# Moving three sums of raw weight blocks per set from VectorE to GpSimd in a seven-product matmul

## The chip, the cores and the metric

The kernel runs on one core of a Trainium2 chip. The metric is the device time in microseconds (us) of one execution. Three timed runs of the kernel before gave 2255.5, 2255.51 and 2257.45 us; the median is 2255.51 us. One more execution was taken by the hardware profiler.

## The reference, cut to what matters

One layer of a hybrid decoder on 256 rows of width 2048: a SwiGLU feed-forward block (FFN), a token mixer, a second FFN, each between RMS norms. The change touches only the two FFNs:

```
def swiglu(x, w_gate, w_up, w_down):
    return (jax.nn.silu(x @ w_gate) * (x @ w_up)) @ w_down      # D_FF = 5504 = 43 tiles of 128

h = swiglu(rms_norm(x, ffn1_pre[l]), ffn1_wg[l], ffn1_wu[l], ffn1_wd[l])
x = x + 0.5 * rms_norm(h, ffn1_post[l])
```

All is float32. The weights come from HBM once each.

## The kernel before, in words

Every product of float32 matrices is made of three TensorE products of rounded halves: the weight block is split into `hi` (ScalarE, line 170, a rounding copy) and `lo` (VectorE, line 171, raw minus `hi`), and the matmul adds x_hi·hi, x_hi·lo and x_lo·hi. So each raw tile of 128x1024 that a DMA brings costs one ScalarE instruction, one VectorE instruction and 6 or 12 matmuls. The raw tiles rotate through 12 buffers (`N_RAW`), `hi` and `lo` through 5 buffers each (`N_SPLIT`): ScalarE and VectorE can run ahead of TensorE by no more than 5 tiles.

Most of each FFN is a main stream (`main`, `linear_steps`, lines 315 to 318) of ordinary products. Into it `weave` threads a side stream (`sevens`) at `RATIO` 0.5: after each batch of main matmuls come 6 side matmuls. The side stream computes four blocks of gate columns and one block of up columns of each FFN, ten groups in the kernel, by Strassen's scheme: x and W are cut in 2x2 blocks, and seven block products replace eight. Sums of blocks of x are made once (`new_forms`). Sums of blocks of W must be made as the weights arrive.

A group has two phases, each over four sets s = 0..3 (a set is two rows of 128 of the contraction). Phase one takes products 1 and 2, on plain blocks. Phase two loads three raw tiles per set, r[0], r[1], r[2] (blocks 11, 12 and 22 of W), on SP's queue (`loads`, line 412) and takes five products. Each product is written s-wise, and a sort key `5*s + d` sets the order: 3(s), 5(s), 4(s-1), 6(s), 7(s). Their operands:

- 3(s): r[2] as loaded
- 5(s): r[0] + r[1], summed into r[0]
- 6(s): that plus r[2], summed into r[0] once 5(s) has been split
- 7(s): r[2] + r[1], summed into r[2]
- 4(s): r[0] of 6(s) plus block 21, added by a DMA with accumulation that GpSimd's queue issues (`t4`, line 454), once 6(s) has been split

The three sums are the function `add`, line 398, on VectorE: 3 per set, 12 per group, 120 in the kernel. The set after the current one is always being loaded (`while len(got) < ...`).

Within the program order the tile framework fixes each engine's queue before the run: it lists instructions by priority (program order) and by when it estimates that their operands are ready. So a sum whose tiles are estimated to have landed can stand in its engine's queue ahead of work of an earlier phase. The queue is then taken strictly in order on the chip. GpSimd's queue holds, in this stretch, the DMAs of `t4` and the DMAs that write partial sums of the down product (lines 648 and 650).

Of the kernel before, what the change touches and what calls it, by code (L numbers as in the profile page):

```python
# [14 lines left out]
ALU = mybir.AluOpType  # L15
# [41 lines left out]
def layer(ctx: ExitStack, tc: tile.TileContext, a, out: bass.AP):  # L57
    nc = tc.nc
    V, S, G, PE = nc.vector, nc.scalar, nc.gpsimd, nc.tensor
# [12 lines left out]
    def slot(shape, dt=F32, s="s"):  # L72
        return pool.tile(shape, dt, tag="slot", bufs=N_SLOT, name=nm(s))
# [10 lines left out]
    def acc(w):  # L84
        return psp.tile([P, 512], F32, tag="bank", bufs=N_BANK, name=nm("acc"))[:, :w]
# [82 lines left out]
    def split(hi, lo, src):  # L168

        S.activation(hi, src, AF.Copy)  # L170
        V.tensor_tensor(lo, src, f32(hi), ALU.subtract)  # L171
# [19 lines left out]
    def raw_tile():  # L191
        return pool.tile([P, 1024], F32, tag="raw", bufs=N_RAW, name=nm("raw"))

    def split_tiles():
        return (pool.tile([P, 1024], F32R, tag="whi", bufs=N_SPLIT, name=nm("whi")),
                pool.tile([P, 1024], F32R, tag="wlo", bufs=N_SPLIT, name=nm("wlo")))
# [193 lines left out]
    def sevens(forms, groups, done):  # L390

        a, b = slice(0, 512), slice(512, 1024)
        fetch, got = [], []

        def add(x, y):
            V.tensor_tensor(x, x, y, ALU.add)  # L398
            return x

        def source(W, col):
            def src(i, j, s):
                k = 8 * i + 2 * s
                return W[k * P:(k + 2) * P, col + 512 * j:col + 512 * j + 512].rearrange("(k p) c -> p k c", p=P)

            return src

        def loads(src, blocks, s):
            tiles = []
            for i, j in blocks:  # L410
                x = raw_tile()
                nc.sync.dma_start(out=x.rearrange("p (k c) -> p k c", c=512), in_=src(i, j, s))
                tiles.append(x)
            return tiles

        for _, W, col, _ in groups:
            for blocks in (((0, 0), (1, 0)), ((0, 0), (0, 1), (1, 1))):
                for s in range(4):
                    fetch.append((source(W, col), blocks, s))

        def phase(first, plan):

            bank = {}
            seen = {p: 0 for p, _, _ in plan}
            for _, p, s, operand in sorted((len(plan) * s + d, p, s, o) for s in range(4) for p, d, o in plan):
                while len(got) < min(first + s + 2, len(fetch)):
                    got.append(loads(*fetch[len(got)]))
                x = operand(s, got[first + s])
                hi, lo = split_tiles()
                split(hi, lo, x)  # L430
                if p not in bank:
                    bank[p] = acc(512)
                ah, al = forms[p]
                for i in range(2):
                    k, ws = 2 * s + i, slice(512 * i, 512 * i + 512)
                    PE.matmul(bank[p], ah[:, k, :], hi[:, ws], start=(seen[p] == 0), stop=False)  # L436
                    PE.matmul(bank[p], ah[:, k, :], lo[:, ws], start=False, stop=False)  # L437
                    PE.matmul(bank[p], al[:, k, :], hi[:, ws], start=False, stop=(seen[p] == 7))  # L438
                    seen[p] += 1
                yield p if seen[p] == 8 else 0, bank[p]  # L440

        for g, (name, W, col, evac) in enumerate(groups):
            src = source(W, col)
            c0, c1 = slot([P, 1024], F32, "sg"), slot([P, 1024], F32, "sg")

            for p, ps in phase(8 * g, [(1, 0, lambda s, r: r[0]), (2, 1, lambda s, r: r[1])]):
                if p == 1:
                    S.activation(c1[:, a], ps, AF.Copy)
                elif p == 2:
                    V.tensor_tensor(c0[:, a], c1[:, a], ps, ALU.add)  # L450
                yield 6

            def t4(s, r):
                G.dma_start(out=r[0].rearrange("p (k c) -> p k c", c=512), in_=src(1, 0, s), accum_op=ALU.add)  # L454
                return r[0]

            for p, ps in phase(8 * g + 4, [(3, 0, lambda s, r: r[2]), (5, 1.1, lambda s, r: add(r[0], r[1])),
                                           (6, 2.2, lambda s, r: add(r[0], r[2])), (7, 3.3, lambda s, r: add(r[2], r[1])),
                                           (4, 6.4, t4)]):
                if p == 5:  # L460
                    m5 = ps
                elif p == 3:
                    m3 = ps
                elif p == 6:
                    V.tensor_tensor(c1[:, a], c1[:, a], ps, ALU.subtract)
                    V.tensor_tensor(c1[:, b], c1[:, a], m5, ALU.add)
                    V.tensor_tensor(c0[:, b], c1[:, b], m3, ALU.add)
                elif p == 7:
                    V.tensor_tensor(c1[:, b], c1[:, b], ps, ALU.add)
                    V.tensor_tensor(c1[:, a], c1[:, a], ps, ALU.add)  # L470
                elif p == 4:
                    V.tensor_tensor(c1[:, a], c1[:, a], ps, ALU.add)
                yield 6
            evac([c0, c1])
            done.add(name)
# [112 lines left out]
    def ffn(u, r, first, then, head, wg, wu, wd, gpost, resid, keep, gname, final, unscale=None):  # L588
# [107 lines left out]

        done = set()
        weave(main(), sevens(forms, groups, done), done, RATIO)
        run_soon()
        y = [[slot([P, 1024], F32, "y") for _ in range(2)] for _ in range(2)]  # L700
# [97 lines left out]
    first = Weights(KD, [(W["ffn1_wg"], 0, 512), (W["ffn1_wg"], 512, 512)])  # L798
# [377 lines left out]
    y = [[slot([P, 1024], F32, "ym") for _ in range(2)] for _ in range(2)]  # L1176
    begin, chunk, post, u2, st2, _, sc2 = closer(y, a["mix_post"], 1.0, x1, x2, "ffn2_pre", None, sq1)
# [43 lines left out]
```

## Time and profile before

| | |
|---|---|
| timed runs, median | 2255.51 us |
| profiled execution's own time | 2245.08 us |
| span of its instructions | 2242.9 us |
| PE (TensorE matmul) busy | 2200.5 us, 98% |
| DVE (VectorE) busy | 1562.9 us, 70% |
| ACT (ScalarE) busy | 1220.2 us, 54% |
| POOL (GpSimd) busy | 138.7 us, 6% |

Times in the rows are microseconds from the span's start unless marked ns. DVE, ACT, POOL and SP are the engines VectorE, ScalarE, GpSimd and SyncE; a `q` behind a name is the engine's own instruction queue. In a row `<-` in brackets gives the idle time of the engine just before the instruction and what ended it. The two FFNs' woven stretches lie at about 112 to 672 us and 1590 to 2146 us.

### The profile page before, as it was taken

To read this page: it belongs to the slowest core of one execution; us is meant where nothing else is said; L and a number is where in the kernel's file an instruction comes from. 1 tells how busy PE (TensorE), PEld (TensorE's weight loads), DVE (VectorE), ACT (ScalarE), POOL (GpSimd) and SP (SyncE) were. 2 spreads that over 40 slices of the span, in tenths; PEclk is the share of its full clock that TensorE was granted. 3 is DMA by queue.
4 is the path that set the end of the run, shared out by engine and by line. 5 is a ranking of instruction groups with operands and counts; after the bars stand their busy time and mean duration, and the time that the engine had idled before them with its cause. 6 is when DMAs were issued, how large, how long until landed. Compare 5 with 4: busy or idle time off the path is not lost.

```text
span 2242.9 us, 28536 instructions
## 1 busy us (share of the span) xinstructions
PE 2200.5 (98%) x10434; PEld 1870.2 (83%) x10434; DVE 1562.9 (70%) x1859; ACT 1220.2 (54%) x1560; POOL 138.7 (6%) x177
## 2 busy tenths in 40 slices
PE   8999999999999999999999999999999999999997
PEld 6888888888887799999888888887888888878886
DVE  6786876878686758686555545558777868687766
ACT  7665655555554654545444444456655555555544
POOL 1001001010011000000000000000010000100110
PEclk9999999999999999999999999999999999999999
DMA  8578788888888464556655566655778788987881
GB/s 326 160 245 255 247 236 265 245 257 248 254 235 314 151 209 127 154 158 183 195 180 196 187 196 202 230 195 186 250 238 260 230 265 243 263 246 239 234 315 55
DMA packets 229244, 497.40 MB, mean 222 GB/s; under 512 B 18360, under 2 KB 51344, under 8 KB 229104
## 3 DMA queue, kind: packets, MB, share of 16 engines
q1 hardware_dynamic: 203456, 436.32, 58.7%
q0 software_dynamic: 25472, 59.20, 12.3%
q8 instruction: 81, 1.33, 0.2%
q14 instruction: 59, 0.48, 0.1%
q10 hardware_dynamic: 176, 0.07, 0.0%
HBM read 472.44 MB, written 23.07 MB: 221 GB/s over the span
## 4 chain that ended last, share of the span: by engine, by line
PE 36%; issue 9%; DVE 3%; DMA 3%; ACT 1%; POOL 0%; DVEq 0%; POOLq 0%; ACTq 0%
PE acc L316 11%; PE acc L318 11%; PE acc L315 11%; DVE wlo L171 2%; DMA raw<-in_ffn_wg_dram 1%; PE acc L438 1%; PE acc L436 1%; PE acc L437 1%; DMA raw<-in_ffn_wu_dram 1%; DMA raw<-in_ffn_wd_dram 1%; PE tp L177 1%; ACT whi L170 0%; DVE raw L398 0%; POOL ysum L650 0%; DVE y L563 0%
## 5 line engine op out<-in xcount | busy, mean ns | idle before, releaser
L171 DVE TENSOR_TENSOR wlo<-raw,whi 128x1024 fp32r<-128x1024 f32 (+2 forms) x937 | 1087.1, 1180 | 479.3 <-ACT whi L170 460.5
L170 ACT ACTIVATE whi<-raw 128x1024 fp32r<-128x1024 f32 (+2 forms) x937 | 951.2, 1027 | 781.9 <-PE acc L318 577.4
L316 PE MATMUL acc<-wlo,uh 128*128 128x512 f32 (+1 forms) x1620 | 600.3, 371 | 5.8 <-DVE wlo L171 5.8
L315 PE MATMUL acc<-whi,uh 128*128 128x512 f32 (+1 forms) x1620 | 605.0, 374 | 0.0
L318 PE MATMUL acc<-whi,ul 128*128 128x512 f32 (+1 forms) x1620 | 524.5, 371 | 0.0
L316 PEld LDWEIGHTS acc<-wlo,uh 128*128 128x128 f32 x1620 | 304.5, 188 | 49.9 <-DVE wlo L171 8.6
L315 PEld LDWEIGHTS acc<-whi,uh 128*128 128x128 f32 x1620 | 304.7, 188 | 41.8 <-ACT mv L791 0.3
L318 PEld LDWEIGHTS acc<-whi,ul 128*128 128x128 f32 x1620 | 301.5, 188 | 41.2
L316 PE MATMUL acc<-wlo,hh 128*128 128x512 f32 x688 | 268.3, 390 | 4.1 <-DVE wlo L171 4.1
L315 PE MATMUL acc<-whi,hh 128*128 128x512 f32 x688 | 268.1, 390 | 0.0
L318 PE MATMUL acc<-whi,hl 128*128 128x512 f32 x688 | 259.4, 389 | 0.0
L398 DVE TENSOR_TENSOR raw<-raw,raw 128x1024 f32<-128x1024 f32 x120 | 146.6, 1221 | 91.5 <-DMA raw<-in_ffn_wg_dram 65.9
L316 PEld LDWEIGHTS acc<-wlo,hh 128*128 128x128 f32 x688 | 129.2, 188 | 32.6 <-DVE wlo L171 6.0
L315 PEld LDWEIGHTS acc<-whi,hh 128*128 128x128 f32 x688 | 129.2, 188 | 26.9
L318 PEld LDWEIGHTS acc<-whi,hl 128*128 128x128 f32 x688 | 129.2, 188 | 26.6
L436 PE MATMUL acc<-whi,sh 128*128 128x512 f32 x320 | 126.6, 396 | 0.0
L438 PE MATMUL acc<-whi,sl 128*128 128x512 f32 x320 | 125.1, 391 | 0.0
L437 PE MATMUL acc<-wlo,sh 128*128 128x512 f32 x320 | 124.8, 390 | 0.0
L437 PE MATMUL acc<-wlo,uh 128*128 128x512 f32 x240 | 93.7, 390 | 1.5 <-DVE wlo L171 1.5
L436 PE MATMUL acc<-whi,uh 128*128 128x512 f32 x240 | 94.6, 394 | 0.5 <-ACT whi L170 0.5
L438 PE MATMUL acc<-whi,ul 128*128 128x512 f32 x240 | 93.6, 390 | 0.0
L454 POOL DMA_DIRECT2D raw<-in_ffn_wg_dram x32 | 38.8, 1213 | 652.0 <-DVE wlo L171 558.6
(323 smaller groups left out, 1911.3 us busy)
## 6 DMA issues: line engine op xcount, KB each, us to landing
raw<-in_ffn_wg_dram SPq DMA_DIRECT2D x192, 512.0 KB, 5.4
raw<-in_ffn_wd_dram SPq DMA_DIRECT2D x172, 512.0 KB, 5.9
raw<-in_ffn_wu_dram SPq DMA_DIRECT2D x168, 512.0 KB, 5.2
raw<-in_w_gate_dram SPq DMA_DIRECT2D x96, 512.0 KB, 4.3
raw<-in_w_in_dram SPq DMA_DIRECT2D x192, 192.0 KB, 2.7
raw<-in_ffn_wg_dram POOLq DMA_DIRECT2D x32, 512.0 KB, 8.2
ysum<-part POOLq DMA_DIRECT2D x64, 256.0 KB, 6.8
raw<-in_w_o_dram SPq DMA_DIRECT2D x32, 512.0 KB, 4.5
```

The costliest lines, as they stand in the source:

```text
L170: S.activation(hi, src, AF.Copy)
L171: V.tensor_tensor(lo, src, f32(hi), ALU.subtract)
L177: PE.transpose(p[:, i, :], src[:, i * P:(i + 1) * P], ident)
L315: PE.matmul(ps[t][c], lh, wh[:, sl], start=(k == 0), stop=False)
L316: PE.matmul(ps[t][c], lh, wl[:, sl], start=False, stop=False)
L318: PE.matmul(ps[t][c], ll, wh[:, span[c]], start=False, stop=(k == nk - 1))
L398: V.tensor_tensor(x, x, y, ALU.add)
L436: PE.matmul(bank[p], ah[:, k, :], hi[:, ws], start=(seen[p] == 0), stop=False)
L437: PE.matmul(bank[p], ah[:, k, :], lo[:, ws], start=False, stop=False)
L438: PE.matmul(bank[p], al[:, k, :], hi[:, ws], start=False, stop=(seen[p] == 7))
L454: G.dma_start(out=r[0].rearrange("p (k c) -> p k c", c=512), in_=src(1, 0, s), accum_op=ALU.add)
```

## The change

The function `add` becomes a GpSimd instruction. The operands of 5(s) and 7(s) are made together by a new step `t13` that stands in the plan without a product (`None`) at key -1.5, that is behind 7(s-1) and ahead of 3(s): first r[0] += r[1], then r[1] += r[2]. So the sum for 7 now lies in r[1] and r[2] stays as loaded. The third sum, r[0] += r[2] for 6(s), stands right behind 5(s). The `None` entries yield no matmuls, and they take their tiles from those already loaded. The products keep their order.

```
         def add(x, y):
-            V.tensor_tensor(x, x, y, ALU.add)
-            return x
+            G.tensor_tensor(x, x, y, ALU.add)
...
-            seen = {p: 0 for p, _, _ in plan}
-            for _, p, s, operand in sorted((len(plan) * s + d, p, s, o) for s in range(4) for p, d, o in plan):
+            seen = {p: 0 for p, _, _ in plan if p is not None}
+            for _, p, s, operand in sorted(((len(seen) * s + d, p, s, o) for s in range(4) for p, d, o in plan),
+                                           key=lambda e: e[0]):
+                if p is None:
+                    operand(s, got[first + s])
+                    continue
...
+            def t13(s, r):
+                add(r[0], r[1])
+                add(r[1], r[2])
+
-            for p, ps in phase(8 * g + 4, [(3, 0, lambda s, r: r[2]), (5, 1.1, lambda s, r: add(r[0], r[1])),
-                                           (6, 2.2, lambda s, r: add(r[0], r[2])), (7, 3.3, lambda s, r: add(r[2], r[1])),
-                                           (4, 6.4, t4)]):
+            for p, ps in phase(8 * g + 4, [(None, -1.5, t13), (3, 0, lambda s, r: r[2]), (5, 1.1, lambda s, r: r[0]),
+                                           (None, 1.2, lambda s, r: add(r[0], r[2])), (6, 2.2, lambda s, r: r[0]),
+                                           (7, 3.3, lambda s, r: r[1]), (4, 6.4, t4)]):
```

## Rows read from the trace of the kernel before

**Rows 1.** The page, part 1: busy time of each engine.

```profile
PE 2200.5 (98%) x10434; PEld 1870.2 (83%) x10434; DVE 1562.9 (70%) x1859; ACT 1220.2 (54%) x1560; POOL 138.7 (6%) x177
```

**Rows 2.** Two woven stretches: length, busy us (instructions) of each engine, clock, DMA.

```profile
112.00:672.00 560.00, 557.75 (x2509) 463.20 (x2508) 426.13 (x397) 319.07 (x346) 48.38 (x51) 1.00 0.83 249
1590.00:2146.00 556.00, 549.97 (x2478) 456.93 (x2477) 419.57 (x391) 313.88 (x339) 50.68 (x54) 1.00 0.83 246
```

**Rows 3.** Line 398, the sums: ns min/median/max, first and last start.

```profile
L398 DVE TENSOR_TENSOR raw<-raw,raw x120: 1210/1224/1228, 127.7 to 2137.1; 128x1024 f32<-128x1024 f32 x120
```

**Rows 4.** Timeline of PE: start, us, instruction, idle before it and its releaser.

```profile
384.36 0.50 PE L316 MATMUL acc<-wlo,uh 128*128 128x512 f32 x1 [0.96 <-DVE wlo L171]
...
1846.14 0.50 PE L316 MATMUL acc<-wlo,uh 128*128 128x512 f32 x1 [0.76 <-DVE wlo L171]
...
1964.54 0.50 PE L316 MATMUL acc<-wlo,hh 128*128 128x512 f32 x1 [1.90 <-DVE wlo L171]
...
2084.59 0.50 PE L316 MATMUL acc<-wlo,hh 128*128 128x512 f32 x1 [2.20 <-DVE wlo L171]
```

**Rows 5.** Timeline of DVE, then of ACT, about the last of these waits.

```profile
2075.13 1.23 DVE L171 TENSOR_TENSOR wlo<-raw,whi 128x1024 fp32r<-128x1024 f32 x1 [1.19 <-ACT whi L170]
2082.17 1.22 DVE L398 TENSOR_TENSOR raw<-raw,raw 128x1024 f32<-128x1024 f32 x1 [5.82 <-DMA raw<-in_ffn_wu_dram]
...
2087.32 1.22 DVE L398 TENSOR_TENSOR raw<-raw,raw 128x1024 f32<-128x1024 f32 x1
...
2077.32 2.01 ACT L170 ACTIVATE whi<-raw 128x1024 fp32r<-128x1024 f32 x2
2080.84 1.06 ACT L170 ACTIVATE whi<-raw 128x1024 fp32r<-128x1024 f32 x1 [1.51 <-PE acc L318]
2088.66 1.06 ACT L170 ACTIVATE whi<-raw 128x1024 fp32r<-128x1024 f32 x1 [6.76 <-DVE raw L398]
```

**Rows 6.** Timeline of DVE: four more sums that waited for a load.

```profile
264.49 1.23 DVE L398 TENSOR_TENSOR raw<-raw,raw 128x1024 f32<-128x1024 f32 x1 [3.12 <-DMA raw<-in_ffn_wg_dram]
...
381.94 1.22 DVE L398 TENSOR_TENSOR raw<-raw,raw 128x1024 f32<-128x1024 f32 x1 [4.58 <-DMA raw<-in_ffn_wg_dram]
...
1843.72 1.22 DVE L398 TENSOR_TENSOR raw<-raw,raw 128x1024 f32<-128x1024 f32 x1 [4.37 <-DMA raw<-in_ffn_wg_dram]
...
1962.13 1.23 DVE L398 TENSOR_TENSOR raw<-raw,raw 128x1024 f32<-128x1024 f32 x1 [5.51 <-DMA raw<-in_ffn_wg_dram]
```

**Rows 7.** Timeline of PE: the first matmul of 6(0) in the same five groups.

```profile
276.63 0.47 PE L436 MATMUL acc<-whi,sh 128*128 128x512 f32 x1
...
391.06 0.39 PE L436 MATMUL acc<-whi,sh 128*128 128x512 f32 x1
...
1852.88 0.39 PE L436 MATMUL acc<-whi,sh 128*128 128x512 f32 x1
...
1973.99 0.39 PE L436 MATMUL acc<-whi,sh 128*128 128x512 f32 x1
...
2094.04 0.39 PE L436 MATMUL acc<-whi,sh 128*128 128x512 f32 x1
```

**Rows 8.** GpSimd's add at the kernel's end, and VectorE's line 563 beside it.

```profile
2228.43 1.76 POOL L561 TENSOR_TENSOR y<-y,xr 128x512 f32<-128x512 f32 x1 [70.74 <-ACT y L560]
...
2227.62 3.11 DVE L563 SCALAR_TENSOR_TENSOR y<-y,sm,xr 128x512 f32<-128x512 f32 x3
...
L563 DVE SCALAR_TENSOR_TENSOR y<-y,sm,xr x14: 744/746/1778, 760.8 to 2237.1; 128x512 f32<-128x512 f32 x14
```

**Rows 9.** The DMA of `t4(1)` in the group at 384: sum ahead, issue, use, landing.

```profile
405.08 1.23 DVE L398 TENSOR_TENSOR raw<-raw,raw 128x1024 f32<-128x1024 f32 x1 [1.61 <-DMA raw<-in_ffn_wg_dram]
...
407.74 1.20 POOL L454 DMA_DIRECT2D raw<-in_ffn_wg_dram  x1 [15.50 <-DVE wlo L171]
...
428.75 0.39 PE L436 MATMUL acc<-whi,uh 128*128 128x512 f32 x1
...
DMA to landing us min/median/max: 5.6/8.4/11.0
```

## The prediction

> **What bounds the kernel now.** I read the page's busy line first [rows 1]: TensorE is busy 98% of the span, so whatever is saved on VectorE counts only where TensorE waits for it. Next the stretches in which the seven products are woven in, which are the only ones that the change touches [rows 2]: TensorE is busy 557.75 of 560 us in the first FFN and 549.97 of 556 in the second. The most that any change of the side stream can win there is 2.25 + 6.03 = 8.3 us; VectorE, at 426 of 560 us, has slack. Last I looked on TensorE's timeline for what made it wait inside them. Four of the waits end with a VectorE split [rows 4]: 0.96 + 0.76 + 1.90 + 2.20 = 5.82 us. The timeline of VectorE shows their cause [rows 5]: a sum of line 398 stands at the head of its queue and waits 5.82 us for a load, while splits behind it could run: ScalarE had finished two `hi` tiles at 2079.33 (2077.32 + 2.01) and one at 2081.90. The other three sites look alike, with waits of 4.58, 4.37 and 5.51 us [rows 6]. So VectorE is late there because it takes its queue in order, not because it is busy.
>
> **The change part by part.** Removed from VectorE: 120 sums of 1.224 us [rows 3], 146.9 us, 73.4 in each stretch. I cost this at nothing: TensorE's stream hides it (557.75 of 560 busy), and ScalarE and VectorE already run ahead to the limit of their five tiles; ScalarE's tile at 2080.84 waited for a matmul to release a buffer [rows 5]. If that cover were gone, VectorE's load would be the cost; see the third rival.
>
> The wait leaves VectorE too. Set 2's first sum, the one at 2082.17, now blocks GpSimd's queue, and the splits behind it can run from 2077 on. That is worth the four TensorE waits, -5.82 us.
>
> Added on GpSimd: 120 adds of 128x1024. The trace has no such instruction; the nearest is an add of half the size, 1.76 us from 2228.43 to 2230.19 [rows 8]. Beside it VectorE ran three instructions that take 0.746 us at the median; the longest of the group took 1.778. Put last of the three, it began near 2227.62 + 3.11 - 1.78 = 2228.95, and ended 0.54 us behind GpSimd's add. Read so, GpSimd waited for the second and VectorE's third for GpSimd, and the add itself took 2230.19 - 2228.95 = 1.24 us. Twice that is 2.5 us for our size; twice the whole span is 3.5; VectorE's own 1.22 [rows 3] is the floor. I take 2.75: the 2.5, and 0.25 for waiting behind a split (VectorE without sums is busy 353 of 560 us, half a split is 0.61, together 0.38; two sums of three meet it, since the first begins when VectorE has caught up).
>
> The Trainium skill gives another price. "GPSIMD Engine Reference", section "Performance versus the Vector engine", measures a two-input float32 add of 2048 elements at 4497 ns, about 2.25 us for ours as an estimate; no run here shows one of that size. With it the sum below would come to -4.3 us.
>
> What is late next is 6(0). Its sum stands in GpSimd's queue behind both sums of t13(2), if the order of VectorE's queue holds there: before, set 2's first sum (2082.17) stood ahead of 6(0)'s (2087.32) [rows 5]. Behind it wait ScalarE's `hi` and all behind that; already ScalarE sat 6.76 us for this sum, to 2088.66. Counting from X, the moment at which set 2's load is in: three adds, then `hi` 1.06 and `lo` 1.23, so 3 x 2.75 + 2.29 = 10.54 us. TensorE wants 6(0), if it has not waited before, at its start less X less the wait removed [rows 4 to 7]:
>
> - 391.06 - 381.94 - 0.96 = 8.16, late by 2.38
> - 1852.88 - 1843.72 - 0.76 = 8.40, late by 2.14
> - 1973.99 - 1962.13 - 1.90 = 9.96, late by 0.58
> - 2094.04 - 2082.17 - 2.20 = 9.67, late by 0.87
>
> Together 5.97 us. Of the other four groups whose set 2 comes late, the tightest has 276.63 - 264.49 = 12.14 us and is in time; in the first group of each FFN the loads are in long before. So the sum is -5.82 + 5.97 = +0.15 us. At 2.5 us an add (9.79) the lateness is 1.63 + 1.39 + 0 + 0.12 = 3.14 and the sum -2.7; at 3.5 (12.79) it is 4.63 + 4.39 + 2.83 + 3.12, with 0.65 of the tightest other group 15.6, and the sum +9.8; at the floor of 1.22 (5.95) nothing is late and it is -5.8.
>
> The queue that is moved past is GpSimd's. t13(3) can come ahead of t4(1)'s DMA: in the group at 384 the DMA would go out at 405.08 + 5.5 = 410.6 in place of 407.74 [rows 9]. With the longest landing, 11.0 us, and 2.29 for the split it is ready at 423.9; TensorE takes it at 428.75. At 3.5 us an add it is 425.4. I cost it at nothing; that cover of 3 to 5 us is what it would eat. t4(3), issued last in a group, has no such sum ahead of it. The DMAs of down's partial sums can wait behind two adds, 5.5 us; five buffers stand in front of them. GpSimd's load, 48.4 + 60 x 2.75 = 213 of 560 us, leaves room. SP's loads stay; r[2] comes free with 6(s)'s sum and r[1] with 7(s)'s split, the reverse of before: nothing.
>
> The sum is made against the profiled execution, 2245.08 us, and gives 2245.2. The median of the timed runs lies 10.4 us above that execution; carried over, 2255.7, so I say 2256.
>
> **The rivals.** Faster: 6(0) comes in time, because the second sum of t13(2) stands behind 6(0)'s in GpSimd's queue (two adds ahead of the split, 5.5 + 2.29 = 7.79 us, under all four) or an add takes 2.5 or less. The four waits go and nothing comes: -2.7 to -5.8, about 2250. For it: r[2] is the set's last load. Against: on VectorE set 2's sum led 6(0)'s by 5.15 us (2082.17 to 2087.32), time for two adds.
>
> Slower: the adds take 3.1 us and more, so that 6(0) is late by more than the freed waits gave. Place: 6(0) in the eight groups of [rows 6] and their like. It costs from 2.75 us on; at 3.1 (11.59) the lateness is 3.43 + 3.19 + 1.63 + 1.92 = 10.2, a loss of 4.4; at 3.5 it is +9.8, 2265. For it: 1.76 us of span for half the size [rows 8]. Against: part of that span was waiting.
>
> Port: VectorE and GpSimd hold each other up. In [rows 8] VectorE's instruction stretched from 0.75 to 1.78 us beside GpSimd's. If every sum held VectorE for its full length, VectorE would need 353 + 60 x 3.5 = 563 of 560 us in the first stretch and 346 + 210 = 556 of 556 in the second: about +3 us in the one, level in the other, with the lead of five tiles gone, beside the +9.8 of such adds: some +13, 2268. At 2.5 it is 503 of 560 and TensorE feels nothing. The decisive point is an add of 3.45 us, all of it in VectorE's way.
>
> The rule of this stands in the Trainium skill, "SBUF — State Buffer", section "Who interferes with whom": a VectorE instruction with two SBUF inputs and a GpSimd instruction that reads SBUF exclude each other, each held for the other's whole length. The row of 1.778 us agrees; by it both the splits of line 171 and these adds are of the kind that collide.
>
> That the change doesn't do what it says would be a queue order in which t13 is no set ahead; then 5(s) and 7(s) would need GpSimd's adds in place of VectorE's, 1.5 us longer each, which the lead hides.
>
> **How the numbers follow.** A measurement of this kernel tells 0.2%, 4.5 us, from no change. Forecast (gain and lateness cancel, within 4.5 us): 0.42. Faster rival beyond 4.5 us: 0.27, since it needs nearly all of 5.82. Slower 0.21 and port 0.10, together 0.31. Range 2249 to 2268: the low end is the faster rival's 2249.7 with a little for other waits (8.3 us at most), the high end the port's price; the forecast's own is 2251 to 2260.
>
> **What would show it.** Right: line 398 on GpSimd, near 2.75 us; the four waits of [rows 4] gone; in their groups, near 391, 1853, 1974 and 2094, short waits of TensorE for the split of 6(0), ScalarE ahead of it waiting for GpSimd; the mean of line 171 longer, TensorE's busy time in the two stretches as before. Wrong: no wait at 6(0) (the faster rival), adds of 3.1 us and more, TensorE waiting in many sets instead of the first, or ScalarE waiting for t4(1)'s DMA inside a group.

## The result and the profile after

Measured side by side, eight runs each, the changed kernel takes 2271.78 us at the median and the kernel before 2253.91. The ratio is 1.0075, 95% interval 1.0053 to 1.0098: some 17 us slower, where "no change" was forecast and the range ended at 2268. The two profiled executions stand further apart: 2269.47 us (span 2267.7) against 2245.08 (2242.9).

The page of the changed kernel: the busy line, then the rows of the splits and of the moved sums (busy us, mean ns of one | idle before).

```profile
PE 2210.0 (97%) x10434; PEld 1875.3 (83%) x10434; DVE 1598.1 (70%) x1739; ACT 1219.8 (54%) x1560; POOL 477.0 (21%) x297
...
L171 DVE TENSOR_TENSOR wlo<-raw,whi 128x1024 fp32r<-128x1024 f32 (+2 forms) x937 | 1253.6, 1361 | 560.1 <-ACT whi L170 540.9
...
L398 POOL TENSOR_TENSOR raw<-raw,raw 128x1024 f32<-128x1024 f32 x120 | 342.4, 2865 | 632.3 <-DMA raw<-in_ffn_wg_dram 328.2
```

VectorE lost 146.9 us of sums and is still 35 us busier than before [rows 1]: the 937 splits have gone from 1087.1 to 1253.6 us, 166.5 more. The sums take 2.87 us each on GpSimd. All columns of the two stretches of [rows 2], after:

```profile
112.00:672.00 560.00, 547.63 (x2428) 450.71 (x2428) 438.51 (x328) 310.94 (x336) 212.60 (x109) 0.99 0.81 241
1590.00:2146.00 556.00, 544.37 (x2429) 448.65 (x2428) 432.42 (x328) 312.48 (x337) 213.85 (x109) 1.00 0.81 242
```

TensorE lost 10.1 and 5.6 us of busy time in them. VectorE is at 438 of 560 us, far from full, and so is GpSimd. On averages nothing is short. What TensorE waited for has to be found wait by wait.

**A burst.** The timelines about one group's second set, near the wait at 384.36 before [rows 4]: single splits of VectorE, then GpSimd, then PE (start, us, idle before and releaser).

```profile
367.47 2.74 DVE L171 TENSOR_TENSOR wlo<-raw,whi 128x1024 fp32r<-128x1024 f32 x1 [0.62 <-ACT whi L170]
370.14 3.42 DVE L171 TENSOR_TENSOR wlo<-raw,whi 128x1024 fp32r<-128x1024 f32 x1
373.48 4.22 DVE L171 TENSOR_TENSOR wlo<-raw,whi 128x1024 fp32r<-128x1024 f32 x1
377.61 3.40 DVE L171 TENSOR_TENSOR wlo<-raw,whi 128x1024 fp32r<-128x1024 f32 x1
...
366.11 6.36 POOL L398 TENSOR_TENSOR raw<-raw,raw 128x1024 f32<-128x1024 f32 x2 [11.11 <-DMA raw<-in_ffn_wg_dram]
372.41 1.75 POOL L658 DMA_DIRECT2D ysum<-part  x2
373.56 6.36 POOL L398 TENSOR_TENSOR raw<-raw,raw 128x1024 f32<-128x1024 f32 x2
...
371.13 0.39 PE L440 MATMUL acc<-whi,uh 128*128 128x512 f32 x1
...
375.21 0.39 PE L440 MATMUL acc<-whi,uh 128*128 128x512 f32 x1
...
377.75 0.50 PE L316 MATMUL acc<-wlo,hh 128*128 128x512 f32 x1 [0.79 <-DVE wlo L171]
...
381.07 0.50 PE L316 MATMUL acc<-wlo,hh 128*128 128x512 f32 x1 [1.65 <-DVE wlo L171]
```

GpSimd waits 11.11 us for a load and then runs four adds nearly back to back. In that time VectorE finishes four splits, from 367.47 to 381.01: 13.54 us, 3.4 each, against 1.22 before. TensorE takes two tiles, one of the main and one of the side stream, in the 4.08 us from 371.13 to 375.21, one in 2.04 on average. So VectorE falls 13.54 - 4 x 2.04 = 5.4 us behind. TensorE waits 0.79 + 1.65 = 2.44 of it; the other 3.0 must have been the lead, the tiles that VectorE had split ahead (a difference, not a row). The burst at 1844 does the same (waits of 1.33 and 1.66 at 1855.23 and 1858.55).

**6(0).** The same engines 20 us later, GpSimd, ScalarE and PE; it answers to the 8.16 us of [rows 6, 7].

```profile
391.78 2.38 POOL L398 TENSOR_TENSOR raw<-raw,raw 128x1024 f32<-128x1024 f32 x1 [7.50 <-DMA raw<-in_ffn_wg_dram]
394.11 0.86 POOL L658 DMA_DIRECT2D ysum<-part  x1
394.73 5.01 POOL L398 TENSOR_TENSOR raw<-raw,raw 128x1024 f32<-128x1024 f32 x2
...
397.43 5.98 ACT L170 ACTIVATE whi<-raw 128x1024 fp32r<-128x1024 f32 x6 [7.73 <-POOL raw L398]
...
400.88 0.50 PE L441 MATMUL acc<-wlo,sh 128*128 128x512 f32 x1 [1.83 <-DVE wlo L171]
...
1878.53 0.50 PE L441 MATMUL acc<-wlo,sh 128*128 128x512 f32 x1 [1.84 <-DVE wlo L171]
```

GpSimd's queue is blocked for 7.50 us by a load of set 2, as forecast; behind it stand a DMA issue of down's partial sums and 6(0)'s sum, and ScalarE sits 7.73 us until that sum is made.

**The longest split.** VectorE, GpSimd and PE in the last group of the first FFN:

```profile
630.99 6.17 DVE L171 TENSOR_TENSOR wlo<-raw,whi 128x1024 fp32r<-128x1024 f32 x1
...
631.07 5.00 POOL L398 TENSOR_TENSOR raw<-raw,raw 128x1024 f32<-128x1024 f32 x2
...
637.22 0.50 PE L316 MATMUL acc<-wlo,hh 128*128 128x512 f32 x1 [2.28 <-DVE wlo L171]
```

One split spans two adds from end to end, 6.17 us in place of 1.22, and TensorE waits 2.28 us for it. At 2114.69 it waits 2.17 us for a split of 3.40 that began beside an add.

**The sum.** Waits of TensorE over 0.3 us in the two FFNs (112 to 720, 1590 to 2200) come to 16.5 us before and 31.8 after. The rows of the granted clock hold four pieces at half speed, 17.06 us in all, apart from the kernel's end, against two of 3.41 before (one of them at 7.5 us, ahead of the first clock row of the changed kernel), which costs about (17.06 - 6.82) / 2 = 5.1 us. One of the four pieces, behind the wait that ends at 279.31, in a table of short stretches (columns as in [rows 2]):

```profile
276.00:280.00 4.00, 2.12 (x12) 1.54 (x11) 4.00 (x5) 2.12 (x2) 1.25 (x1) 1.00 0.94 286
280.20:283.40 3.20, 3.20 (x9) 2.43 (x9) 2.52 (x4) 1.46 (x2) 0.00 (x0) 0.50 1.06 241
283.60:287.00 3.40, 3.40 (x17) 2.75 (x17) 2.61 (x2) 1.06 (x1) 2.26 (x1) 1.00 0.83 301
```

TensorE was busy 2.12 of 4 us; right after, its granted clock is 0.50 (1.2 of 2.4 GHz), and it runs 9 matmuls in 3.2 us where it runs 17 in 3.4 later. Waits and clock together are 15.3 + 5.1 = 20.4 of the span's 24.8 us. The other 4.4 lie in TensorE's busy time, which rose by 9.5 us for the same 10434 matmuls, 5.1 of them the clock; no single row has them.

The 31.8 us, wait by wait: eight waits stand right behind lengthened splits, the four of the two bursts, 2.28 and 2.17, and 0.98 and 1.04 at 144.48 and 1624.78 (there an evacuation of line 630 stands in VectorE's queue behind four splits that took 9.03 us): 11.9 us in all. Four hang on a ScalarE that sat for 6(0)'s sum: 1.83 and 1.84, and 1.88 and 1.35 at 279.31 and 1758.95, evacuations again: 6.9 us. The other 13.0 us are mostly the groups' ends; before, 10.7 us were left without the four of [rows 4]. So -5.8 + 6.9 + 11.9 + 2.3 = 15.3.

### The profile page after: what moved, and what is told of

Read it like the earlier page. It is cut to its first block, busy times and chain, and to the rows that moved or that the text cites. A ratio compares the mean times of both kernels' runs of the same rounds, so it can differ in the third digit from the quotient of the medians.

```text
span 2267.7 us, 28648 instructions
## 1 busy us (share of the span) xinstructions
PE 2210.0 (97%) x10434; PEld 1875.3 (83%) x10434; DVE 1598.1 (70%) x1739; ACT 1219.8 (54%) x1560; POOL 477.0 (21%) x297
## 3 DMA queue, kind: packets, MB, share of 16 engines
q8 instruction: 81, 1.33, 0.2%
## 4 chain that ended last, share of the span: by engine, by line
PE 41%; DVE 4%; DMA 3%; issue 3%; POOL 1%; ACT 1%; DVEq 0%; POOLq 0%; ACTq 0%
PE acc L316 11%; PE acc L318 11%; PE acc L315 11%; DVE wlo L171 3%; DMA raw<-in_ffn_wg_dram 2%; PE acc L441 2%; PE acc L442 2%; PE acc L440 2%; POOL raw L398 1%; PE tp L177 1%; ACT whi L170 1%; DMA raw<-in_ffn_wu_dram 0%; DVE y L571 0%; DVE sg L671 0%; DVE ym L571 0%
## 5 line engine op out<-in xcount | busy, mean ns | idle before, releaser
L171 DVE TENSOR_TENSOR wlo<-raw,whi 128x1024 fp32r<-128x1024 f32 (+2 forms) x937 | 1253.6, 1361 | 560.1 <-ACT whi L170 540.9
L398 POOL TENSOR_TENSOR raw<-raw,raw 128x1024 f32<-128x1024 f32 x120 | 342.4, 2865 | 632.3 <-DMA raw<-in_ffn_wg_dram 328.2
L441 PEld LDWEIGHTS acc<-wlo,sh 128*128 128x128 f32 x320 | 60.5, 189 | 15.8 <-DVE wlo L171 4.3
```

Source lines behind the costliest of these rows:

```text
L398: G.tensor_tensor(x, x, y, ALU.add)
```

## The experiments

Three theories stood. **Port**: a GpSimd add and a VectorE split, which both read SBUF, hold each other up, and back-to-back adds eat the lead. **Queue**: GpSimd's queue is taken in order, so 6(0)'s sum stands behind set 2's sums and their loads. **Order**: the new order of the sums is bad by itself, whichever engine makes them. Ratios below are to the kernel before on the same chip.

**order_dve**: the changed kernel, its sums on VectorE.

```
         def add(x, y):
-            G.tensor_tensor(x, x, y, ALU.add)
+            V.tensor_tensor(x, x, y, ALU.add)
```

> The new plan as it is, with all three sums back on VectorE. Known before it runs: the changed kernel is 17.9 us slower than the one before (2271.78 against 2253.91), its profiled run waits for splits and for line 630, and splits beside a GpSimd add take 2.45 us in place of 1.22. Port theory (VectorE and GpSimd hold each other up, and adds that stand back to back on GpSimd let VectorE do one split for each add): no GpSimd add, no collision, so as before, 2252 to 2257. Queue theory (6(0)'s sum is late behind the sums of set 2, which wait for a load, in GpSimd's queue): the same, since all stand on VectorE again as before, perhaps with longer waits of VectorE for loads, 2254 to 2260. Third theory, that the new order of the sums does the harm by itself: most of the loss stays, 2265 and more.

Measured 1.0111 [1.0092, 1.0130]. Order hit, port and queue missed: without GpSimd the new order is worse still. The instructions of its line 398, and what ended VectorE's idle time ahead of them (us, times):

```profile
L398 DVE TENSOR_TENSOR raw<-raw,raw x120: 1215/1225/1227, 127.7 to 2164.0; 128x1024 f32<-128x1024 f32 x120
...
  DMA raw<-in_ffn_wg_dram: 73.3, 32
  DMA raw<-in_ffn_wu_dram: 29.1, 9
```

and the timeline of VectorE, then of PE, at one of these places:

```profile
386.09 1.23 DVE L398 TENSOR_TENSOR raw<-raw,raw 128x1024 f32<-128x1024 f32 x1 [6.90 <-DMA raw<-in_ffn_wg_dram]
...
388.50 0.80 PE L316 MATMUL acc<-wlo,uh 128*128 128x512 f32 x1 [3.29 <-DVE wlo L171]
```

The sums keep 1.225 us, but VectorE stands 73.3 + 29.1 = 102.4 us at the head of its queue for loads, 6.90 of them just ahead of the wait shown. So the order that asks for sums a set ahead is what needs GpSimd: an engine that makes them must be able to stand still. It says nothing yet of why GpSimd is slow at it.

**six_dve**: the changed kernel, 6(s)'s sum alone on VectorE.

```
-                                           (None, 1.2, lambda s, r: add(r[0], r[2])), (6, 2.2, lambda s, r: r[0]),
+                                           (None, 1.2, lambda s, r: add(r[0], r[2], V)), (6, 2.2, lambda s, r: r[0]),
```

> The changed kernel with only 6(s)'s sum back on VectorE, so that 80 sums stay on GpSimd, in pairs. Queue theory: 6(0) no longer stands behind set 2 in GpSimd's queue, the waits of 1.83 and 1.84 us at 6(0) and those of line 630 behind ScalarE's waits for GpSimd go, at most +5 us over before, about 2257. Port theory: the pairs still collide, two thirds of the lengthened splits stay (some 90 of 136), waits for splits stay, +8 to +14 us, 2262 to 2268.

Measured 1.0019 [1.0007, 1.0031]: queue hit, port missed. The waits at 6(0) are gone, and three quarters of the loss with them. But that edit also takes 40 adds off GpSimd. The bursts are not gone: three groups keep theirs, 7.8 us of TensorE's waits in all. The timelines of VectorE, GpSimd and PE in one:

```profile
1950.34 16.92 DVE L171 TENSOR_TENSOR wlo<-raw,whi 128x1024 fp32r<-128x1024 f32 x7 [0.62 <-ACT whi L170]
...
1948.64 6.70 POOL L398 TENSOR_TENSOR raw<-raw,raw 128x1024 f32<-128x1024 f32 x2 [12.15 <-DMA raw<-in_ffn_wg_dram]
...
1956.43 6.34 POOL L398 TENSOR_TENSOR raw<-raw,raw 128x1024 f32<-128x1024 f32 x2
...
1963.91 0.50 PE L316 MATMUL acc<-wlo,hh 128*128 128x512 f32 x1 [1.65 <-DVE wlo L171]
```

**five_gp**: the kernel before, 5(s)'s sum alone on GpSimd.

```
-            for p, ps in phase(8 * g + 4, [(3, 0, lambda s, r: r[2]), (5, 1.1, lambda s, r: add(r[0], r[1])),
+            for p, ps in phase(8 * g + 4, [(3, 0, lambda s, r: r[2]), (5, 1.1, lambda s, r: add(r[0], r[1], G)),
```

> The kernel before with only 5(s)'s sum on GpSimd: 40 single adds, the ones that made VectorE wait for loads. Port theory: 40 adds in place of 120, one at a time, so a third of the collisions; of the 17.9 us some 3 to 6 stay, less the 5.8 us of the four waits, 2251 to 2255. Queue theory: 6(s)'s sum is on VectorE and waits for nothing new, the four waits go, 2248 to 2250.

Measured 0.9972 [0.9958, 0.9985], faster than both. All four waits of [rows 4] are gone: the gain that the prediction counted on is real, and 40 adds, one per set, bring it. They take 2.45 us at the median, and stretch splits too (1140.5 us in all on the page), but stand singly: no two start within 5.1 us.

**fill**: the changed kernel, each sum replaced by two fills of the same tile; the sums are left out.

```
         def add(x, y):
-            G.tensor_tensor(x, x, y, ALU.add)
+            G.memset(x, 1.0)
+            G.memset(x, 0.5)
```

> The changed kernel with each GpSimd add replaced by two fills of the same tile with a constant: GpSimd writes SBUF and reads none; the sums are left out, so the weights of products 4 to 7 are wrong. GpSimd's queue, its order and the waits for loads stay, with shorter work if two fills take less than the add's 2.4 us. Port theory: a fill does not read, the splits stay at 1.22 us, and most of the loss goes, 2252 to 2258. Queue theory: 6(0)'s place in GpSimd's queue behind set 2 stays, and with it most of the loss if two fills take about 2 us, 2262 to 2270.

Measured 0.9957 [0.9942, 0.9973]: queue missed, port right in direction and exceeded. Tiles and plan are the changed kernel's; GpSimd only writes, and is done in about 1.9 us. The queue is the changed kernel's as far as 6(0), but not behind it, as fill_three shows below, and a fill waits only for the load of the tile that it writes. Its line 171 (ns at the least, median, most):

```profile
L171 DVE TENSOR_TENSOR wlo<-raw,whi x937: 898/1226/1228, 6.2 to 2211.9; 128x1024 fp32r<-128x1024 f32 x159, 128x768 fp32r<-128x768 f32 x26, 128x774 fp32r<-128x774 f32 x3
```

and one of the two fills on its page:

```profile
L399 POOL MEMSET raw<- 128x1024 f32 x120 | 114.7, 960 | 5.6
```

No split is longer than 1.228 us; in the changed kernel the longest is 6.175. But two things differ from the adds beside the queue, the reading and the length; fill_three keeps the length.

**five_three**: five_gp with an add, a subtraction and an add in place of each add on GpSimd (120 instructions, always three in a row).

```
-            V.tensor_tensor(x, x, y, ALU.add)
+            eng.tensor_tensor(x, x, y, ALU.add)
+            if eng is G:
+                G.tensor_tensor(x, x, y, ALU.subtract)
+                G.tensor_tensor(x, x, y, ALU.add)
```

> The faster kernel (only 5(s)'s sum on GpSimd, 0.9972 of before) with that sum done in three GpSimd instructions on the same tiles, add, subtract, add: 120 GpSimd instructions of this kind as in the changed kernel, back to back in threes, but 6(s)'s and 7(s)'s sums on VectorE. Port theory: bursts of three collide as in the changed kernel, one VectorE split of 2.5 to 3.2 us for each, TensorE waits for splits during the bursts; 10 to 18 us over the faster kernel, 1.002 to 1.006 of before. Queue theory: nothing that TensorE needs soon stands behind them (5(s) is summed one or two sets ahead), so as fast as the faster kernel, 0.996 to 0.999.

Measured 1.0329 [1.0307, 1.0350]. Port had the direction and not the size, 10 to 18 us over five_gp where some 80 came; queue had neither. The same number of GpSimd instructions as in the changed kernel, all in runs of three, costs over four times as much. The splits on its page:

```profile
L171 DVE TENSOR_TENSOR wlo<-raw,whi 128x1024 fp32r<-128x1024 f32 (+2 forms) x937 | 1301.5, 1415 | 467.2 <-ACT whi L170 451.2
```

and the two largest of TensorE's waits (us in total, times, longest):

```profile
PE tp L177 <- DVE sg L625: 31.9, 10, 5.8
PE acc L316 <- DVE wlo L171: 29.3, 23, 3.5
```

The first of these are the evacuations of line 625, VectorE's too. 5(s)'s and 6(s)'s operands come two adds later as well, so this run prices runs of adds and late operands together, not the port alone.

**old_plan_gp**, **six_gp** and **five_seven_gp**: the order of the kernel before, with all three sums, with 6(s)'s, or with 5(s)'s and 7(s)'s on GpSimd. The first two as diffs, the third is like them:

```
+                                           (6, 2.2, lambda s, r: add(r[0], r[2], G)), (7, 3.3, lambda s, r: add(r[2], r[1], G)),
...
+                                           (6, 2.2, lambda s, r: add(r[0], r[2], G)), (7, 3.3, lambda s, r: add(r[2], r[1])),
```

> The kernel before with all three sums on GpSimd and nothing else changed: 7(s)'s sum goes into r[2] and has to wait for 3(s), so that only 5(s)'s sums, 40, can stand ahead, one for each set and none in pairs. Port theory: 120 collisions, but scattered; a few us over before, 1.000 to 1.003. Queue theory: 6(0) stands behind one sum of set 2 in place of two (2 x 2.75 + 2.29 = 7.8 us, in time by the prediction's table), so no lateness and the four waits freed, 0.997 to 0.999. If the loss of the changed kernel were in the number of GpSimd adds alone, 1.0075 as there.

Measured 1.0113 [1.0095, 1.0132]; all missed. Without the set ahead each product waits for its own add: ScalarE waits 62.0 us in 24 places for GpSimd. The splits are lengthened as much as in the changed kernel (1254.9 us on the page, after 1253.6).

> The kernel before with only 6(s)'s sum on GpSimd. VectorE's sums of 5(s) still wait for loads, so the four waits of TensorE stay. Queue theory: nothing stands ahead of 6(s)'s sum on GpSimd; it takes 2.75 in place of 1.22 us, 1.5 late at 6(0) of the two tightest groups at most: 1.000 to 1.002. Port theory: 40 single collisions, 1.000 to 1.002 as well. Both fail if it is over 1.004: then a GpSimd add on the way from 5(s) to 6(s) costs by itself.

Measured 1.0063 [1.0040, 1.0086]; both missed, and by a third cause. 7(s)'s sum on VectorE writes r[2], which GpSimd's sum for 6(s) still reads, so VectorE stands at the head of its queue for GpSimd (us, times):

```profile
  POOL raw L398: 60.9, 26
```

The run therefore says nothing of queue or port; it is a wait that the edit itself made, and one that the change avoids by leaving r[2] as loaded.

> The kernel before with 5(s)'s and 7(s)'s sums on GpSimd and 6(s)'s on VectorE: the same 80 sums as in the run with 6(s) on VectorE (1.0019), but 7(s)'s waits for 3(s) and can't stand beside 5(s)'s. Port theory: no pairs and no bursts of four, so the waits of 0.75 to 1.67 us for splits at the end of a group's first phase go; 0.997 to 1.000. Queue theory: 7(0)'s sum stands behind 5(2)'s wait for a load, the lateness moves from 6(0) to 7(0), a step later and so mostly hidden: 0.998 to 1.002.

Measured 1.0014 [1.0002, 1.0026]; queue hit, port missed by little. Eighty adds, but only six pairs that start within 4.3 us of each other, and burst waits of no more than 0.41 us; what is left are waits at the ends of groups (2.94 us at 579.25 at the most). So the same 80 sums cost about as much without bursts as with them in six_dve (1.0019): the burst waits went, the ends took their place.

**fill_three**: the changed kernel with three fills per sum, 2.85 us, the length of an add; the sums are left out.

```
         def add(x, y):
-            G.tensor_tensor(x, x, y, ALU.add)
+            G.memset(x, 1.0)
+            G.memset(x, 0.25)
+            G.memset(x, 0.5)
```

> The changed kernel with each GpSimd add replaced by three fills of the same tile (sums left out, products 4 to 7 get constants): at 0.95 us a fill, as the run with two fills showed, GpSimd is busy for 2.85 us per sum, the 2.87 us that the adds took on average, in the same queue order and behind the same waits for loads, but it reads no SBUF. In the run with two fills (1.9 us per sum) the loss was gone, 0.9957. Queue theory: with the adds' own length 6(0) is late again as in the changed kernel, waits of about 1.8 us at 6(0) and at line 630, 8 to 12 us over the run with two fills, 1.000 to 1.002. Port theory: what made the chain late were the splits held up beside the adds and the adds held up beside splits; no reading, no collision, 0.995 to 0.998.

Measured 1.0008 [0.9992, 1.0024]: queue hit, port missed. GpSimd is as busy as in the changed kernel (212.79 us in the first stretch, after 212.60) and reads nothing. Its line 171:

```profile
L171 DVE TENSOR_TENSOR wlo<-raw,whi x937: 897/1224/1228, 6.7 to 2225.5; 128x1024 fp32r<-128x1024 f32 x159, 128x768 fp32r<-128x768 f32 x26, 128x774 fp32r<-128x774 f32 x3
```

and the timelines of ScalarE and PE in the group shown above:

```profile
388.38 5.80 ACT L170 ACTIVATE whi<-raw 128x1024 fp32r<-128x1024 f32 x6 [7.83 <-POOL raw L400]
...
390.76 0.50 PE L443 MATMUL acc<-wlo,sh 128*128 128x512 f32 x1 [0.76 <-DVE wlo L171]
...
413.18 0.66 PE L177 MATMUL tp<-ident,sg 128*128 128x128 f32 x4 [3.29 <-DVE sg L632]
```

No split is stretched, and no wait for a split of the main stream is longer than 0.41 us. But the large wait, 3.29 at 413.18 (3.47 at 1881.53 in the second FFN), isn't one of the changed kernel's. GpSimd's and ScalarE's timelines ahead of it:

```profile
403.62 1.84 POOL L398 MEMSET raw<- 128x1024 f32 x2 [11.41 <-DMA raw<-in_ffn_wg_dram]
...
409.07 3.90 ACT L170 ACTIVATE whi<-raw 128x1024 fp32r<-128x1024 f32 x4 [7.60 <-POOL raw L400]
```

Here the framework has put a fill that ScalarE needs next, by its place 6(1)'s, behind a load of set 3. In the changed kernel 6(1)'s add, at 407.73, runs ahead of set 3's, at 415.24. So the differences between these runs are no clean prices: from fill to fill_three 1.0008 - 0.9957 = 0.51%, some 11.5 us, for length and this order together; from fill_three to the changed kernel, at the same length, 1.0075 - 1.0008 = 0.67%, some 15 us (0.3 to 1.1% by the ends of the two intervals; the two were not timed side by side), for the reading, less these two waits that only fill_three has. What the fills show without the order is that splits stay short beside a GpSimd that writes as long and doesn't read, and that the eight waits behind lengthened splits, 11.9 us in the changed kernel's profile, are gone.

**five_late4**: five_gp, with product 4(2) moved behind 7(3), since the ends of the groups were five_gp's last waits. **late4_dve** is that move alone, all sums on VectorE; **five_gp_again** repeats five_gp beside the first of them.

```
-            for _, p, s, operand in sorted((len(plan) * s + d, p, s, o) for s in range(4) for p, d, o in plan):
+            for _, p, s, operand in sorted((len(plan) * s + d + (2.1 if (p, s) == (4, 2) else 0), p, s, o)
+                                           for s in range(4) for p, d, o in plan):
```

> The faster kernel (5(s)'s sum alone on GpSimd) with product 4(2) put behind 7(3), so that the DMA of t4(3) has one product and one main batch more, 4.1 us, before 4(3) needs it. In the faster kernel's profile the ends of the last two groups of each FFN still wait for it: 2.28 and 1.22 us of TensorE in the first, 2.20 and 0.35 in the second, with a stretch at 1.2 GHz behind the one of 2.20. If these waits are the DMA's, they go: 4 to 8 us, 0.994 to 0.996 of before. If they come of the order of the evacuations behind it, nothing changes: 0.997.

> The faster kernel once more, unchanged, on the same chip as the run above for a direct comparison: 0.996 to 0.9985 of before.

> The kernel before with one edit: product 4(2) comes behind 7(3), all three sums stay on VectorE. It asks whether the best version's gain is the sum of two separate ones. Moving 5(s)'s sum alone gave 0.997; both edits together 0.9904. If the two add up, 4(2)'s move alone gives 0.9904/0.997 = 0.9934 (0.992 to 0.995), about 15 us, the waits of TensorE at the ends of the groups (577.6 and its like) gone, the four waits for VectorE's split at sets 2 still there. If the move pays only once VectorE's blocked queue is out of the way (because 7(3) and 4(2) follow late splits), it gives 0.997 to 1.000.

Measured 0.9904 [0.9883, 0.9925], 0.9970 [0.9954, 0.9985] and 0.9956 [0.9937, 0.9975]. The repeat hit. five_late4, at 2230.35 us against 2250.59, beats both kernels and its own forecast; the two parts multiply to 0.9972 x 0.9956 = 0.9928, which agrees once the intervals of all three are counted. late4_dve came near its forecast of 0.9934, but two, not four, of the waits at set 2 were left (2.76 us at 386.23 and 1.19 at 1849.35): the sums at the head of VectorE's queue there waited 6.38, 4.80, 1.52 and 2.59 us for loads, in place of 4.58, 4.37, 5.51 and 5.82. The stretches of [rows 2] in five_late4:

```profile
112.00:672.00 560.00, 560.00 (x2524) 466.40 (x2523) 435.90 (x380) 324.94 (x350) 100.80 (x72) 1.00 0.84 250
1590.00:2146.00 556.00, 555.70 (x2517) 464.11 (x2516) 430.27 (x379) 320.39 (x343) 103.67 (x80) 1.00 0.85 250
```

TensorE is busy 1115.70 of 1116 us there, so 8.0 of the 8.3 us that the prediction called the most that the side stream can win have been won. That ceiling was too low: the kernel before has another 8.3 us of waits just behind the two stretches, from 688 to 704 and from 2155 to 2171, at the last groups' ends. Of the 14.1 us between the profiled spans (2242.9 to 2228.8), 12.8 are waits over 0.3 us that are gone, 16.5 to 3.7.

## Why the prediction was wrong

The forecast was +0.15 us; the medians say +17.9, the profiled executions +24.4. Step by step:

- **Sums off VectorE at no gain, four waits freed, -5.82**: right as a mechanism. With no reading on GpSimd and short operations (fill) the kernel is 9.7 us faster than before, more than the 5.82. In the changed kernel the gain is eaten: new waits stand at 377.75, 381.07, 1855.23 and 1858.55, near the first two of [rows 4], and for a new reason.
- **An add at 2.75 us**: 2.87 at the mean, 2.38 at the least. Good enough: it moves the sum to +1.6 by the prediction's own formula, and 2.85 to +1.4.
- **6(0) late by 2.38, 2.14, 0.58 and 0.87, together 5.97**: 1.83 and 1.84 in the two tightest groups, nothing at 6(0) in the other two. For the two the place and the size were right, the composition not: 6(0)'s sum stood behind one sum of set 2, not two, and in the missing add's place came a DMA issue (394.11) and a split stretched from 1.23 to 2.30 us. What was missed is that the work behind 6(0) is late too: at 279.31 and 1758.95, in groups that were called in time, TensorE waited 1.88 and 1.35 us for evacuations after ScalarE had sat 5.27 and 4.68 us for 6(0)'s sum. The total, 6.9 us, is near 5.97 partly by luck. So is fill_three's 1.8 us over before (interval -1.8 to +5.4) against the formula's +1.4: its waits lay elsewhere, 0.76 us at 6(0) and 3.29 at 413.18.
- **t4's DMAs at nothing**: the sums did not delay the last of a group, as forecast. The waits at two groups' ends still grew, from 1.28 to 2.53 us and from 1.13 to 1.52. In the first of them the time from the issue of t4(3)'s DMA to ScalarE's `hi` went from 8.23 us (564.11 to 572.34) to 9.46 (573.87 to 583.33), 1.23 more: the landing, not the queue.
- **The port**, the step that failed: "At 2.5 it is 503 of 560 and TensorE feels nothing", and from it "The decisive point is an add of 3.45 us". VectorE was indeed far from full, 439 of 560 us. The reasoning failed. Adds don't come spread over the stretch; they come as loads land, four in 14 us, and in those 14 us VectorE needs 3.4 us per split against TensorE's 2.04 per tile. Only the lead, 3.0 us there, stands between that and a wait. Outside the bursts a single split that spanned two adds was enough for a wait of 2.28. The balance to draw was over the burst, as the result's section does. By the prediction's own prices a pair takes 2.5 + 1.22 = 3.7 us and four pairs put VectorE 4 x (3.7 - 2.04) = 6.6 us behind; a full lead of five tiles, 10.2 us, would have covered that, so the lead as it really stood was needed as well, and it was not looked up. This term, which was set to zero, measures 11.9 us of waits in the profiled run; by the runs' difference it is some 15 us, with the limits told under fill_three.
- **TensorE's clock and pace**, no term of the sum: 5.1 us of clock, and 4.4 us more of busy time.

The port rival named the right mechanism and had a chance of 0.10. That its 2268 us is near the measured time is luck: it was made of adds of 3.5 us and a VectorE full over the whole stretch, and neither came. The rule behind it stands in the Trainium skill, "SBUF — State Buffer", section "Who interferes with whom", which has a VectorE instruction with two SBUF inputs contend with a GpSimd instruction that reads SBUF and not with one that only writes it. This case agrees on both halves: in the burst beside adds the splits take 3.4 us, beside fills 1.22. The prediction named this rule and priced it over a stretch.

Left open: how the timed runs' 17.9 us split, since the terms above are those of the profiled executions, 24.4 us apart; how much of the clock's 5.1 us each wait brought, since no run could hold the clock; why the split at 373.48 took 4.22 us and not 3.4, and the one at 630.99 6.17; and 4.4 us of busy time.

## What to carry to other kernels

Price contention between two engines over the shortest burst in which the one works without pause, against the lead that the consumer has there, not over a stretch: 78% busy hid a rate 1.7 times too slow. Work moved to another engine's in-order queue brings its waits with it, so move what can wait and leave behind what is needed next; here one sum of three was worth 0.3%, and all three cost 0.75%. Spread operations that exclude each other singly between the other's instructions, since pairs use the lead up (waits of up to 1.67 us behind bursts in six_dve, 0.41 at the most in five_seven_gp); old_plan_gp shows that this alone isn't enough when each operand then comes late.

## What the runs showed of the hardware

- A 128x1024 float32 add takes GpSimd 2.38 us at the least, and up to 3.49 in the changed kernel; a fill of that size takes 0.95 us. The estimate of 2.25 us worked out from the Trainium skill, "GPSIMD Engine Reference", section "Performance versus the Vector engine", is 5.5% below the fastest add of the changed kernel.
- An add and a split that meet hold each other: in the burst the adds took 3.0 to 3.3 us and the splits 2.7 to 4.2. One split lasted 6.17 us, over two whole adds. A GpSimd instruction that only writes left all 937 splits of fill and fill_three at 1.228 us or less.
- After waits of 1.88 and 2.28 us (279.31, 637.22) the granted clock was 0.50 for 3.41 us; after those of 1.83, 1.84, 2.17 and 2.53 at 400.88, 1878.53, 2114.69 and 588.64 no such piece follows. So the length of the wait alone does not tell it.
